# Two-layer attention and short-convolution encoder on one core: main stage of each layer put in a written order on three engines, first modulation in pairs of chunks

## The chip, the cores and the metric

The kernel runs on one core of a Trainium2 chip. The time is device microseconds of one execution. The kernel before took 310.88 us (median of three runs, 310.80 to 311.26).

## The reference

Two layers act on x (256 rows of 1024). In each layer, c (one row) is turned into a shift, a scale and a gate; x is normalised by its root mean square, scaled and shifted; one product with w_in (1024 by 4096) gives queries, keys, values and a gate for eight heads of 64, and four parts u, b, c, g of a convolution; both branches go through one product with w_out, are normalised again, gated and added to x:

```python
    for l in range(DEPTH):
        mod = c_act @ w_ada[l] + b_ada[l]
        shift, scale, gate = jnp.split(mod, 3, axis=-1)
        h = rms_norm(x, pre_norm_g[l]) * (1.0 + scale[:, None, :]) + shift[:, None, :]
        proj = h @ w_in[l]
        ...
        att = dilated_attention(q, k, v, rel_bias).astype(h.dtype) * jax.nn.silu(g_att)
        cnv = b_gate * short_conv(c_gate * u, conv_w[l]) * jax.nn.silu(g_conv)
        mix = jnp.concatenate([att, cnv], axis=-1) @ w_out[l]
        x = x + gate[:, None, :] * rms_norm(mix, post_norm_g[l])
```

Everything is fp32. In the kernel the three dilated windows become one additive bias over all 256 keys.

## The kernel before

**Products.** A large product is made of three (`mm3`, lines 234 to 239): each operand is split into a high part (a cast on ScalarE, line 145) and the rest (a subtraction on VectorE, line 146), and high by high, high by low and low by high are added in PSUM. Small products (sums for the modulation, transposes, probabilities by values) are left in plain fp32.

**First stage (layer 0, lines 413 to 506).** The order on TensorE, ScalarE and VectorE is the program's own here (`manual_schedule`). It goes over eight chunks k of 128 input columns: a row of w_in (0.92 MB, line 394) and chunk k of shift and scale from w_ada (two transfers of 0.52 MB, line 256) are loaded; `sums` (16 products, line 295, with c on 32 columns in four corners of the array) and `columns` (line 314) give the shift and scale of chunk k; `modulate` writes that chunk of h; then q, k, v and a part of the gate get their share. Within one chunk's turn the order is "q0 q1 sums k0 cols k1 g v", where sums and cols are those of the next chunk. Chunk k+1 can begin only when its cols are there.

**Main stage (lines 513 to 707 for both layers).** `split_heads` (lines 359 to 370) takes queries and keys out of PSUM for both heads of a pair. Then chunks of 256 columns of w_in are projected (u, c, b, g, a in layer 0; q, k, u, c, g, b, a in layer 1), each followed by its use; `attend(h)` (line 523) makes the scores of a head (lines 528, 529), the soft maximum (lines 534, 537), the division (lines 540, 542), four transposes (line 546), a copy to SBUF (line 548, by turns VectorE and ScalarE) and, for an odd head, the products of both heads with the values (line 554). Beside that `mods_task` makes the modulation of layer 1 and `gate_task` the gate of this layer; three of these seven sums are gathered on VectorE (`vector_sums`, lines 279 to 281) with eight short fp32 products at the end (line 287), the others on TensorE. The modulation of layer 1 is turned round through SBUF by four small transfers and one transpose (lines 569, 575). This stage has no written order: a scheduler with a timeline of its own orders each engine's queue, with heads first (`high_priority`), so splits can run ahead as far as six buffers allow.

**Between the layers (lines 757 to 811)** the order is again the program's: the last products of w_out, the second norm, the residual and the values of layer 1.

Of the kernel before, what the change touches and what calls it, by code (L numbers as in the profile page):

```python
# [10 lines left out]
F32 = mybir.dt.float32  # L11
# [4 lines left out]
P = 128  # L16
S = 256
# [51 lines left out]
def encoder_kernel(ctx, tc, x, c, w_ada, b_ada, pre_g, w_in, conv_w, rel_bias, w_out, post_g, rows, out):  # L69
# [40 lines left out]
    ones = const.tile([P, 32], F32, name="ones")  # L110
# [42 lines left out]

    def load_behind(l, c0):

        with tc.issue_after(mod_act.ins), tc.issue_after(mod_dve.ins):
            return load_cols(l, c0)
# [100 lines left out]

    def set_mods(l, k0, cols):
# [12 lines left out]
    def vector_sums(raws, pool, tag):  # L272

        for kk in range(KC // 2):
            for kh in range(2):
                k = kk + kh * (KC // 2)
                for raw in raws:
                    if kk == 0:
                        nc.vector.tensor_scalar_mul(raw[:, k], raw[:, k], c_rep[:, k, 0:1])
                    else:  # L280
                        nc.vector.scalar_tensor_tensor(raw[:, k], raw[:, k], c_rep[:, k, 0:1], raw[:, k - 1],  # L281
                                                       op0=ALU.mult, op1=ALU.add)
        g_ps = pool.tile([P, raws[0].shape[-1]], F32, name=tag)
        for kh in range(2):
            for t in range(2):
                j = 2 * kh + t
                nc.tensor.matmul(g_ps[32 * j:32 * j + 32, :], ones, raws[t][:, (kh + 1) * (KC // 2) - 1, :], start=True, stop=True)
        return take_sums(g_ps)
# [9 lines left out]
    def take_sums(g_ps, copy=nc.scalar.copy):  # L298
        acc = work.tile(list(g_ps.shape), F32, name="acc", bufs=5)
        copy(acc, g_ps)  # L300
        return acc
# [17 lines left out]
    def gate_rows(l, accs):  # L319
# [4 lines left out]
        b_row, g_row = [work.tile([2, 2, WC], F32, name=n, tag="junk", bufs=3) for n in ("b_row", "g_row")]  # L324
        nc.gpsimd.dma_start(b_row, b_ada[l, 2 * D:3 * D].rearrange("(h q n) -> h q n", h=2, q=2))
        nc.gpsimd.dma_start(g_row, post_g[l].rearrange("(h q n) -> h q n", h=2, q=2))
# [11 lines left out]
    gate_acc = {}  # L338
# [34 lines left out]
    for l in range(DEPTH):  # L373
        if l == 0:
# [38 lines left out]
            with tc.manual_schedule(engines=MANUAL):  # L413
                ada_raw = ada_load(0, 0, 1)
# [13 lines left out]
                acc = sums(ada_raw, ps, "ps", nc.vector.tensor_copy)  # L428
# [9 lines left out]
                for k in range(KC):  # L438
                    (wh, wl), (vh, vl), (gh, gl), to = next_row
                    if k == 0:  # L440
                        set_mods(0, 0, columns(acc, ps, "ps"))
                        for (a, b), w in list(zip(pieces, to))[:LEAD[0]]:
# [31 lines left out]
                    for item in (FIRST_ORDER if first else LAST_ORDER if last else ROW_ORDER).split():  # L474
# [21 lines left out]
                        elif item == "sums":  # L496
                            next_row = row_parts(k + 1)
                            acc = sums(ada_raw, ps, "ps", nc.vector.tensor_copy if first else nc.scalar.copy)
                            if not first:
                                lead_split(k + 1)  # L500
                        elif item == "lead":
                            lead_split(k + 1)
                        else:
                            set_mods(0, k + 1, columns(acc, ps, "ps"))
                sg0 = act.tile([P, 2, S], F32, name="sg0")
            nc.scalar.copy(sg0, g0_ps)
            nc.scalar.activation(warm, hT_lo[:, KC - 1, 0:1].bitcast(F32), AF.Exp, scale=0.0)
        else:
            w = load_behind(l, 0)
            q_ps = [proj_T(l, i * WC, w if i == 0 else None) for i in range(2)]  # L510
            k_ps = [proj_T(l, AW + i * WC) for i in range(2)]

        if l > 0:
            attention_tiles()
            with tc.issue_after(mod_act.ins), tc.issue_after(mod_dve.ins):
                store_values(v_ps)
        for i in range(2):
            split_heads(i, q_ps[i], k_ps[i])


        pT, turned, taken = {}, {}, {}

        def attend(h):
            o, m = h % 2, h // 2
            s_ps = ps.tile([P, NT, S], F32, name="ps")
            for t in range(NT):
                q = qkv["q"][o][:, m, t * P:(t + 1) * P]
                nc.tensor.matmul(s_ps[:, t, :], q, qkv["k"][:, o, m, :], start=True, stop=False)  # L528
                nc.tensor.matmul(s_ps[:, t, :], q, qkv["k_lo"][:, o, m, :], start=False, stop=True)  # L529
            pr_sb = work.tile([P, NT, S], F32, name="prob", bufs=3)  # L530
            mx = small.tile([P, NT], F32, name="mx", bufs=4)
            sm = small.tile([P, NT], F32, name="sm", bufs=4)
            for t in range(NT):
                nc.vector.tensor_tensor_reduce(pr_sb[:, t, :], s_ps[:, t, :], u[:, h, t * P:t * P + S][:, ::-1], scale=-1.0,  # L534
                                               scalar=3.0e38, op0=ALU.add, op1=ALU.min, accum_out=mx[:, t:t + 1])
            for t in range(NT):
                nc.scalar.activation(pr_sb[:, t, :], pr_sb[:, t, :], AF.Exp, scale=-1.0, bias=mx[:, t:t + 1],  # L537
                                     accum_out=sm[:, t:t + 1])
            rc = small.tile([P, NT], F32, name="rc", bufs=4)
            nc.vector.reciprocal(rc, sm)  # L540
            for t in range(NT):
                nc.vector.tensor_scalar_mul(pr_sb[:, t, :], pr_sb[:, t, :], rc[:, t:t + 1])
            t_ps = ps.tile([P, NT, S], F32, name="ps")
            for t in range(NT):
                for kt in range(NT):
                    turned[h] = nc.tensor.transpose(t_ps[:, kt, t * P:(t + 1) * P], pr_sb[:, t, kt * P:(kt + 1) * P], ident)  # L546
            pT[h] = work.tile([P, NT, S], F32, name="pT", bufs=3)
            (nc.vector.tensor_copy, nc.scalar.copy)[h % 2](pT[h], t_ps)
            if h % 2 == 0:
                return  # L550
            a_ps = ps.tile([P, S], F32, name="ps")
            for kt in range(NT):
                for hh in (h - 1, h):
                    taken[h] = nc.tensor.matmul(a_ps[(hh % 2) * HD:(hh % 2 + 1) * HD, :], qkv["v"][:, kt, hh * HD:(hh + 1) * HD],  # L554
                                     pT[hh][:, kt, :], start=kt == 0, stop=kt == NT - 1)
            nc.scalar.copy(qkv["o"][:, h // 2], a_ps)

        nxt = l + 1 < DEPTH

        if nxt:
            parts = const.tile([32, P], F32, name="parts")
# [266 lines left out]
```

## Time and profile before

| | |
|---|---|
| median of three runs | 310.88 us |
| the profiled execution | 311.03 us, of which the span is 309.3 us |
| TensorE busy | 300.4 us (97%) |
| VectorE busy | 211.8 us (68%) |
| ScalarE busy | 178.1 us (58%) |
| moved by DMA | 72.39 MB, mean 234 GB/s |
| mean granted TensorE clock | 0.997 |

The span runs from the first to the last instruction, 1.7 us less than the execution. Stages can be told apart by the lines that TensorE works on: warming and the first two chunks until 28 us, chunks 2 to 7 until about 65 us, the main stage of layer 0 until 158.8 us, the turn to layer 1 until 184.6 us, its main stage with the output product until 302.8 us, and the end. TensorE's time must be read by starts: a product of 256 columns lasts 0.28 us in the record, but the next one begins 0.117 us after it.

### The profile page before, as it was taken

How to read it: one execution, taken by the hardware profiler on the slowest of the kernel's cores; microseconds unless marked ns; L12 is line 12 of the kernel's file. 1: busy time of each engine (PE TensorE's matmuls, PEld its weight loads, DVE VectorE, ACT ScalarE, POOL GpSimd, SP SyncE). 2: the span in 40 equal slices, each digit the busy share in tenths (PEclk: the TensorE clock that was granted, in tenths of full speed). 3: DMA queues.
4: the chain of work that ended last, by engine and by line, in shares of the span. 5: the costliest groups of instructions: out<-in, count | busy, mean ns of one | idle time of the engine just before them, and what ended most of it. 6: DMA issues, size and time to landing. Idle time of an engine off the chain costs nothing.

```text
span 309.3 us, 6050 instructions
## 1 busy us (share of the span) xinstructions
PE 300.4 (97%) x2421; PEld 261.3 (84%) x2421; DVE 211.8 (68%) x430; ACT 178.1 (58%) x318; POOL 24.1 (8%) x49
## 2 busy tenths in 40 slices
PE   8999999999999999999999999999999999999991
PEld 6878998899877779878677899999998989998881
DVE  3554446589988498688449798798868686845333
ACT  4633445599247243989437584569637695663211
POOL 5220000000000000110013410000000001000011
PEclk9999999999999999999999999999999999999998
DMA  7999999999979999989912399758548632000002
GB/s 244 327 350 330 322 351 343 358 350 348 313 248 344 348 348 323 404 281 351 345 65 66 114 350 344 227 153 242 152 135 272 265 137 70 0 2 0 2 35 102
DMA packets 65692, 72.39 MB, mean 234 GB/s; under 512 B 1778, under 2 KB 61526, under 8 KB 65664
## 3 DMA queue, kind: packets, MB, share of 16 engines
q1 hardware_dynamic: 64512, 70.39, 70.9%
q0 software_dynamic: 784, 1.20, 1.2%
q8 instruction: 19, 0.31, 0.4%
q10 hardware_dynamic: 368, 0.42, 0.4%
q14 instruction: 9, 0.07, 0.1%
HBM read 70.91 MB, written 1.07 MB: 233 GB/s over the span
## 4 chain that ended last, share of the span: by engine, by line
PE 83%; DVE 4%; SPq 4%; DMA 3%; POOL 1%; issue 1%; ACT 1%; POOLq 0%; DVEq 0%; ACTq 0%
PE pm L237 21%; PE pm L238 21%; PE pm L239 21%; PE ps L554 4%; DMA raw<-in_w_in 3%; PE pm L295 3%; PE ps L546 3%; SPq L394 2%; PE ps L295 2%; SPq L256 2%; PE ps L238 2%; PE ps L237 2%; PE ps L239 1%; PE ps L528 1%; PE ps L529 1%
## 5 line engine op out<-in xcount | busy, mean ns | idle before, releaser
L237 PE MATMUL pm<-hT_hi,hi 128*128 128x256 f32 x408 | 116.2, 285 | 0.0
L238 PE MATMUL pm<-hT_lo,hi 128*128 128x256 f32 x408 | 114.9, 282 | 0.1
L239 PE MATMUL pm<-hT_hi,lo 128*128 128x256 f32 x408 | 114.4, 280 | 0.0
L146 DVE TENSOR_TENSOR lo<-raw,hi 128x1024 fp32r<-128x1024 f32 (+1 forms) x94 | 94.0, 1028 | 29.6 <-ACT hi L145 29.2
L145 ACT CAST hi<-raw 128x1024 fp32r<-128x1024 f32 (+1 forms) x94 | 80.5, 893 | 32.9 <-PE pm L238 15.3
L237 PEld LDWEIGHTS pm<-hT_hi,hi 128*128 128x128 f32 x408 | 76.8, 188 | 5.6 <-issue 4.5
L238 PEld LDWEIGHTS pm<-hT_lo,hi 128*128 128x128 f32 x408 | 76.8, 188 | 2.5 <-issue 1.9
L239 PEld LDWEIGHTS pm<-hT_hi,lo 128*128 128x128 f32 x408 | 76.8, 188 | 1.2 <-issue 0.8
L237 PE MATMUL pm<-hi,hT_hi 128*128 128x512 f32 (+1 forms) x68 | 23.7, 348 | 0.0
L239 PE MATMUL pm<-hi,hT_lo 128*128 128x512 f32 (+1 forms) x68 | 23.6, 346 | 0.0
L238 PE MATMUL pm<-lo,hT_hi 128*128 128x512 f32 (+1 forms) x68 | 23.3, 343 | 0.0
L537 ACT ACTIVATE prob<-prob,mx 128x256 f32<-128x256 f32 x32 | 16.0, 503 | 4.0 <-DVE mx L534 3.9
L281 DVE SCALAR_TENSOR_TENSOR raw<-raw,c_rep 128x256 f32<-128x256 f32 x36 | 16.0, 477 | 0.1
L182 ACT ACTIVATE junk<-pm 128x512 f32<-128x512 f32 (+1 forms) x9 | 5.0, 550 | 17.2 <-PE pm L239 17.1
L239 PEld LDWEIGHTS pm<-hi,hT_lo 128*128 128x128 f32 x68 | 12.8, 188 | 2.2 <-DVE hT_lo L231 0.6
L237 PEld LDWEIGHTS pm<-hi,hT_hi 128*128 128x128 f32 x68 | 12.8, 188 | 2.0 <-DVE hT_hi L230 0.4
L724 DVE TENSOR_TENSOR og<-pm,gg 128x512 f32<-128x512 f32 (+1 forms) x9 | 5.6, 630 | 12.7 <-ACT junk L182 12.7
L238 PEld LDWEIGHTS pm<-lo,hT_hi 128*128 128x128 f32 x68 | 12.8, 188 | 1.3
L554 PE MATMUL ps<-pT,v_sb 128*64 128x256 f32 x64 | 13.8, 398 | 0.0
L238 PE MATMUL pm<-lo,mix_a 128*128 128x512 f32 (+1 forms) x36 | 13.4, 373 | 0.0
L237 PE MATMUL pm<-hi,mix_a 128*128 128x512 f32 (+1 forms) x36 | 13.4, 372 | 0.0
L239 PE MATMUL pm<-hi,mix_a 128*128 128x512 f32 (+1 forms) x36 | 12.7, 371 | 0.0
(176 smaller groups left out, 446.0 us busy)
## 6 DMA issues: line engine op xcount, KB each, us to landing
raw<-in_w_in SPq DMA_DIRECT2D x25, 1024.0 KB, 7.6
raw<-in_w_ada SPq DMA_DIRECT2D x16, 1024.0 KB, 10.8
raw<-in_w_ada SPq DMA_DIRECT2D x16, 512.0 KB, 8.4
raw<-in_w_out SPq DMA_DIRECT2D x8, 1024.0 KB, 6.9
raw<-in_w_in SPq DMA_DIRECT2D x7, 896.0 KB, 10.0
u<-t_dr SPq DMA_DIRECT2D x1, 1536.0 KB, 10.0
x_sb<-in_x SPq DMA_DIRECT2D x2, 512.0 KB, 4.3
gg<-r_dr POOLq DMA_DIRECT2D x2, 512.0 KB, 4.2
```

Of the source, the lines that this page charges most:

```text
L145: nc.scalar.copy(hi, raw)
L146: nc.vector.tensor_sub(lo, raw, hi.bitcast(F32))
L237: nc.tensor.matmul(o, ah, bh, start=first, stop=False, **kw)
L238: nc.tensor.matmul(o, ah, bl, start=False, stop=False, **kw)
L239: return nc.tensor.matmul(o, al, bh, start=False, stop=last, **kw)
L256: nc.sync.dma_start(raw[:, t], w_ada[l].rearrange("(k p) n -> p k n", p=P)[:, :, t * D + k0 * P:t * D + (k0 + n) * P])
L281: nc.vector.scalar_tensor_tensor(raw[:, k], raw[:, k], c_rep[:, k, 0:1], raw[:, k - 1], op0=ALU.mult, op1=ALU.add)
L295: nc.tensor.matmul(g_ps[32 * j:32 * j + 32, :], c_rep[:, kk + kh * (KC // 2), :], raws[t][:, kk + kh * (KC // 2), :], start=kk == 0, stop= ...
L394: row_dma[0] = nc.sync.dma_start(raw[:, a:b], w_in[0, k * P:(k + 1) * P, a:b])
L537: nc.scalar.activation(pr_sb[:, t, :], pr_sb[:, t, :], AF.Exp, scale=-1.0, bias=mx[:, t:t + 1], accum_out=sm[:, t:t + 1])
L546: turned[h] = nc.tensor.transpose(t_ps[:, kt, t * P:(t + 1) * P], pr_sb[:, t, kt * P:(kt + 1) * P], ident)
L554: taken[h] = nc.tensor.matmul(a_ps[(hh % 2) * HD:(hh % 2 + 1) * HD, :], qkv["v"][:, kt, hh * HD:(hh + 1) * HD], pT[hh][:, kt, :], start=kt ...
```

## The change

The main stages of both layers get a written order on TensorE, ScalarE and VectorE (SyncE's and GpSimd's queues stay with the scheduler). A chunk is worked in two halves, the units j = 0, 1, 2 and so on (24 in layer 0, 34 in layer 1), each 24 products. For each j the loop emits: sums that are due; the values of a pair (`take`); scores; transposes (`turn`); the division; what `PLAN` lists; the split of unit j+2; the soft maximum; loads; the products of unit j; their use. Head h starts at unit `HEAD_AT[l][h]`; its division comes one unit later, its transposes two, and an odd head's values three. All seven sums are on TensorE; the columns of the modulation of layer 1 come from `columns`, two chunks each time, without the small transfers. All copies of turned probabilities go to ScalarE.

In the first stage shift and scale are loaded and summed for chunks 0, 1, 2+3 and 4+5; for 6+7 VectorE gathers them in eight steps of 512 elements (four after the splits of chunk 4, four after those of chunk 5), and `columns_of` turns the result.

```diff
-GATE_AT = ((0, 3), (None, 1))
-ROWS_AT = (6, 5)
-MODS_AT = (1, 2, 4, 5)
-HEAD_AT = ((2, 2, 3, 4, 5, 6, 6, 7), (0, 0, 1, 2, 3, 4, 5, 6))
+UNITS = ("u0 u1 c0 c1 b0 b1 g0 g1 a1 o0 o1 o2", "q0 k0 q1 k1 u0 u1 c0 c1 g0 g1 b0 b1 a0 a1 o0 o1 o2")
+LOADS = ("u1 c0 s0 c1 b0 s1 b1 r0 g0 s2 g1 r1 a1 s3 o0 o1 o2 o3", "q0 k0 q1 k1 u0 u1 r1 c0 c1 g0 g1 b0 b1 a0 a1 o0 o1 o2 o3")
+HEAD_AT = ((2, 4, 6, 8, 10, 12, 14, 16), (6, 8, 11, 13, 16, 18, 21, 23))
+PLAN = ({0: "=heads0", 1: "=heads1 =copy0", 5: "<sums0", 6: "=cols0", 7: "<sums1", 8: "=cols1 =taps0", 9: "<gate0 =taps1",
+         10: "=taps2", 11: "<sums2 =taps3", 12: "=cols2 =line0", 13: "<gate1", 15: "<sums3", 16: "=cols3 =rows0", 17: "=conv0 >side0",
+         18: "=conv1 =att0", 19: ">att1"},
+        {1: "=store0", 4: "=heads0", 8: "=heads1 =line0", 11: "<gate1", 13: "=rows0", 16: "=taps0", 17: "=taps1", 18: "=taps2",
+         19: "=taps3", 24: "=conv0", 25: "=conv1", 28: "=att0", 29: "=att1"})
+AHEAD = 2
+ADA_GROUPS = ((0, 1, -1), (1, 1, 0), (2, 2, 1), (4, 2, 3), (6, 2, 4))
...
+    def chain(raws, acc):
...
+        for k, (raw, j) in enumerate(steps):
+            part = raw[..., j, :]
+            if k == 0:
+                nc.vector.tensor_scalar_mul(part, part, c_rep[:, k, 0:1])
+            else:
+                nc.vector.scalar_tensor_tensor(acc if k == KC - 1 else part, part, c_rep[:, k, 0:1], before,
+                                               op0=ALU.mult, op1=ALU.add)
...
-                    if k + 1 < KC:
-                        ada_raw = ada_load(0, k + 1, 1)
+                    for f, n, at in ADA_GROUPS[1:]:
+                        if at == k:
+                            ada_raw[f] = ada_load(0, f, n) if f < 6 else ada_halves(0, f)
...
+                    if k in (4, 5):
+                        if k == 4:
+                            last_chain = chain(ada_raw[6], last_acc)
+                        for _ in range(KC // 2):
+                            next(last_chain)
...
-                            acc = sums(ada_raw, ps, "ps", nc.vector.tensor_copy if first else nc.scalar.copy)
+                            if k + 1 in ada_raw and k + 1 < 6:
+                                acc = sums(ada_raw[k + 1], ps, "ps", nc.vector.tensor_copy if first else nc.scalar.copy)
...
-                        else:
+                        elif k + 1 == 6:
+                            set_mods(0, 6, columns_of([last_acc[:, t] for t in range(2)], ps, "ps"))
+                        elif k + 1 in ada_raw:
                             set_mods(0, k + 1, columns(acc, ps, "ps"))
...
+        with tc.manual_schedule(engines=MANUAL):
...
+            def turn(h):
...
+                nc.scalar.copy(pT[h], t_ps)
...
+            for j, (name, m) in enumerate(units):
+                stage = {j - at: h for h, at in enumerate(HEAD_AT[l])}
+                late = PLAN[l].get(j, "").split()
+                for what in [w for w in late if w[0] == "<"]:
+                    does[what[1:-1]](int(what[-1]))
+                if 3 in stage and stage[3] % 2:
+                    take(stage[3])
+                if 0 in stage:
+                    scores(stage[0])
+                if 2 in stage:
+                    turn(stage[2])
+                if 1 in stage:
+                    divide(stage[1])
+                for what in [w for w in late if w[0] == "="]:
+                    does[what[1:-1]](int(what[-1]))
+                if j + AHEAD < len(units):
+                    split_unit(*units[j + AHEAD])
+                if 0 in stage:
+                    softmax(stage[0])
+                load_more()
...
+                    out_unit(name, m)
+                else:
+                    project(name, m)
+                    if m:
+                        use(name)
+                for what in [w for w in late if w[0] == ">"]:
+                    does[what[1:-1]](int(what[-1]))
+            load_more()
+            w1, w2 = [[parts_of[n, m] for m in range(2)] for n in ("o1", "o2")]
+            w = [split(raws["o3"][:, m, :], [P, D]) for m in range(2)]
```

In `PLAN`, heads0 and heads1 are `split_heads(0)` and `split_heads(1)`, unchanged; s0 to s3 are the sums of the modulation of layer 1, r0 and r1 those of the gate, conv and att the splits of the two branches for the output product, copy0 and side0 the copy and the activation of the gate part that the first stage made.

## Rows read from the trace of the kernel before

**Rows 1.** The page: busy time by engine, and the chain that ended last, by engine.

```profile
PE 300.4 (97%) x2421; PEld 261.3 (84%) x2421; DVE 211.8 (68%) x430; ACT 178.1 (58%) x318; POOL 24.1 (8%) x49
...
PE 83%; DVE 4%; SPq 4%; DMA 3%; POOL 1%; issue 1%; ACT 1%; POOLq 0%; DVEq 0%; ACTq 0%
```

**Rows 2.** Stretches: length, busy PE, PEld, DVE, ACT, POOL, PEclk, DMA share, GB/s.

```profile
28.00:61.50 33.50, 33.43 (x357) 29.90 (x358) 18.12 (x44) 15.71 (x33) 0.00 (x0) 1.00 1.10 342
61.50:158.80 97.30, 97.30 (x768) 80.97 (x767) 75.04 (x152) 61.40 (x109) 4.08 (x7) 1.00 0.99 325
...
184.60:280.20 95.60, 95.60 (x783) 89.34 (x782) 72.77 (x136) 62.80 (x101) 1.17 (x2) 1.00 0.51 165
```

**Rows 3.** Timeline of TensorE, first stage: start, us, instruction, idle before in brackets.

```profile
22.90 1.07 PE L295 MATMUL ps<-raw,c_rep 128*32 128x128 f32 x30 [0.16 <-DMA raw<-in_w_ada]
...
27.85 0.39 PE L237 MATMUL pm<-hT_hi,hi 128*128 128x256 f32 x1
28.30 0.38 PE L238 MATMUL pm<-hT_lo,hi 128*128 128x256 f32 x1
...
29.79 1.08 PE L295 MATMUL ps<-raw,c_rep 128*32 128x128 f32 x32
...
31.61 0.28 PE L314 MATMUL ps<-pair,acc 128*128 128x2 f32 x2
```

**Rows 4.** Timeline of TensorE, main stage of layer 0.

```profile
91.86 1.93 PE L295 MATMUL pm<-raw,c_rep 128*32 128x256 f32 x30
...
98.27 0.28 PE L237 MATMUL pm<-hT_hi,hi 128*128 128x256 f32 x1
...
98.50 0.28 PE L239 MATMUL pm<-hT_hi,lo 128*128 128x256 f32 x1
98.71 1.08 PE L554 MATMUL ps<-pT,v_sb 128*64 128x256 f32 x6
```

**Rows 5.** Stretches, busy PE of one line: L295; L287 in both layers; L554.

```profile
61.50:158.80 97.30, 10.19 (x128) 4.20 (x128) 1.00 0.99 325
...
61.50:158.80 97.30, 2.94 (x16) 0.71 (x16) 1.00 0.99 325
184.60:280.20 95.60, 0.64 (x8) 0.16 (x8) 1.00 0.51 165
...
61.50:158.80 97.30, 6.89 (x32) 2.65 (x32) 1.00 0.99 325
```

**Rows 6.** Groups by line and shape: count, busy us, mean ns of one, idle before.

```profile
L146 DVE TENSOR_TENSOR lo<-raw,hi 128x1024 fp32r<-128x1024 f32 x64 | 77.0, 1222 | 21.8 <-ACT hi L145 21.4
...
L145 ACT CAST hi<-raw 128x1024 fp32r<-128x1024 f32 x64 | 65.4, 1050 | 28.6 <-PE pm L238 15.3 <-DMA raw<-in_w_in 7.2 <-PE pm L239 2.2
L537 ACT ACTIVATE prob<-prob,mx 128x256 f32<-128x256 f32 x32 | 16.0, 503 | 4.0 <-DVE mx L534 3.9
...
L534 DVE CUSTOM_DVE_ANT_0 prob<-ps,u 128x256 f32<-128x256 f32 x32 | 12.2, 420 | 0.3
...
L537 ACT ACT_TABLE_LOAD x5 | 6.4, 1283 | 0.1
...
L729 DVE SCALAR_TENSOR_TENSOR x_sb<-og,rstd,x_sb 128x512 f32<-128x512 f32 x7 | 5.0, 748 | 1.5 <-POOL rstd L194 1.5
```

**Rows 7.** Timelines of ScalarE and VectorE, heads of layer 1, idle before in brackets.

```profile
200.73 0.60 ACT L363 ACTIVATE q_odd<-pm 64x512 fp32r<-64x512 f32 x1 [0.93 <-DVE q_even L364]
...
207.18 0.58 ACT L368 CAST k_hh<-pm 64x512 fp32r<-64x512 f32 x1 [1.78 <-DVE k_low L370]
...
215.22 0.69 DVE L370 TENSOR_TENSOR k_low<-pm,k_hh 64x512 fp32r<-64x512 f32 x1 [0.76 <-ACT k_hh L369]
```

**Rows 8.** TensorE's first products (timeline), and a stretch after its last one.

```profile
1.48 3.78 PE L381 MATMUL ps<-zeros 128*128 128x256 f32 x8 [1.48 <-DVE zeros L109]
...
5.39 2.72 PE L381 MATMUL ps<-zeros 128*128 128x256 f32 x8
...
307.00:308.00 1.00, 0.00 (x0) 0.00 (x0) 0.00 (x0) 0.00 (x0) 0.00 (x0) 0.63 0.51 168
```

More of the change, by code (lines that the diff above doesn't have):

```diff
@@ L298, in take_sums @@
     def take_sums(g_ps, copy=nc.scalar.copy):
-        acc = work.tile(list(g_ps.shape), F32, name="acc", bufs=5)
+        acc = work.tile(list(g_ps.shape), F32, name="acc", bufs=6)
         copy(acc, g_ps)
@@ L513, in encoder_kernel @@
[L513 to L544, printed above, removed]
-                for kt in range(NT):
[L546 to L556, printed above, removed]
@@ L609, in encoder_kernel @@
-        running = []
-        step = [0]
-        def side():
-            for h in heads[step[0]]:
-                with tc.high_priority(1000):
-                    attend(h)
-            running.extend(starts[step[0]])
-            step[0] += 1
-            for t in list(running):
-                try:
-                    next(t)
-                except StopIteration:
-                    running.remove(t)
-        def chunk(c0, use, w=None, pool=pm):
-            use(proj_T(l, c0, w, pool))
-            side()
@@ L704, in encoder_kernel, with mix_k @@
-        side()
-        while running or any(starts[step[0]:]) or any(heads[step[0]:]):
-            side()
-        w = load_out(l, OUT_K[3])
+                        out_k(t, parts_of[name, m], k, n, k == OUT_K[0], False)
+            def mix_k(k, ts_):
+                if k < 4:
+                    return hT_hi[:, k, ts_], hT_lo[:, k, ts_]
+                return cv["mix"][:, 0, k - 4, ts_], cv["mix"][:, 1, k - 4, ts_]
+            cuts = [[slice(0, 512), slice(512, 1024)] for _ in range(NT)]
@@ new lines, in encoder_kernel, with out_k, out_pair @@
+            if not nxt:
+                cuts[1][1:] = [slice(512, 768), slice(768, 1024)]
+            def out_k(t, w, k, n, first, last):
+                cs = cuts[t][n]
+                mm3(o_ps[t][n], mix_k(k, slice(t * P, (t + 1) * P)), (w[0][:, cs], w[1][:, cs]), first, last)
+            def out_pair(w, k0, ts):
+                for kk in range(2):
+                    for t in ts:
+                        for n in range(len(cuts[t])):
+                            out_k(t, w[kk], k0 + kk, n, k0 + kk == OUT_K[0], False)
@@ new lines, in heads_in, with lines @@
+            def heads_in(i):
+                if l == 0:
+                    split_heads(i, q_ps[i], k_ps[i])
+                else:
+                    split_heads(i, pending[f"q{i}"], pending[f"k{i}"])
+            def lines(_):
+                cv["lines"] = gate_lines(l)
+            does = {"heads": heads_in, "taps": taps, "conv": conv_split, "att": gate_heads, "sums": mods_sums, "cols": mods_cols,
+                    "gate": gate_sums, "line": lines, "rows": lambda _: gate_rows(l, gates[l], *cv["lines"]),
+                    "copy": lambda _: nc.scalar.copy(sg0, pending["g0"]), "store": lambda _: store_values(pending["v"]),
+                    "side": lambda i: gate_of(i, sg0)}
```

329 lines of the change are left out of this document (189 added, 140 removed).

## The prediction

> **What bounds the kernel now.** I read the page first, then stretches, then the timeline of TensorE by starts. TensorE is busy 97% of the span and holds 83% of the chain that ended last [rows 1]. The stretches show how evenly: from 28 to 158.8 us and from 184.6 to 280.2 us it has no idle time worth naming [rows 2]. In those stretches the records also follow each other without holes: products of 256 columns start 0.117 us apart (two steps from 98.27 to 98.50), and a change between the three-part products and plain fp32 costs about 0.1 us on each side [rows 4]. So only two things can move the time: TensorE's own work, and new waits of TensorE. VectorE (75.0 of 97.3 us in the main stage of layer 0) and ScalarE (61.4) are not full [rows 2]; they matter by the order in which they do things. DMA moves 342 GB/s in the first stage, at a share over 1 [rows 2], and there TensorE already finds one transfer just arriving (0.16 us idle at 22.90) [rows 3].
>
> The sum is made against the profiled execution, 311.03 us (span 309.3), 0.15 above the median.
>
> **First stage, TensorE's work.** Sums of chunks 3, 5, 6 and 7 go: each is 1.0 us and 0.2 for two changes of kind, so -4.8. The sums for 2+3 and 4+5 are twice as wide: by duration 1.93 against 1.08 [rows 3, 4], +0.85 each, +1.7. Columns (0.14 to 0.28 for a pair [rows 3]) are eight turns before and ten after in fewer places: 0. Together -3.1.
>
> **First stage, waits.** (a) The sums for chunk 2 wait for their slice of w_ada. The queue to them now carries 1.05 MB more: 1.05 / 0.342 = 3.1 us [rows 2]. Nothing on TensorE hides it, since that transfer is only just in time today and the sums stand ahead of half of chunk 1's products. Bounds: 0 (the queue had slack) and 3.1; I take 3.0, nearest the row with the idle time. The present 0.16 and the 0.45 at 27.85 (instead of 0.1) [rows 3] go, -0.6: splits and h will be early there. (b) VectorE's chain for chunks 6+7: eight steps of 512 elements at most 0.75 each (the same operation in the residual) [rows 6], 0.7 back to back, 2.8 for four. The second four stand behind the splits of chunk 5, which end about 1.5 us after TensorE starts on that chunk. So they end near 4.3, while TensorE asks for the columns after 18 products, at 2.1: +2.1. Bounds 0 and 3. First stage: -3.1 + 3.0 - 0.6 + 2.1 = **+1.4**.
>
> **Main stages, TensorE's work.** Values: 6.89 us a layer, four pairs, each in two pieces [rows 5]; a piece of six lasts 1.08 [rows 4], so eight in one piece 1.3. Saved 6.89 - 4 x 1.3 = 1.7 a layer. Sums, layer 0: 10.19 + 2.94 today [rows 5] against six of 2.04 (1.93 for 30 instructions [rows 4]): -0.9, and three share their changes of kind with values, -0.6. Columns for layer 1: +1.1, the transpose that goes -0.2. Layer 0: **-2.3**. Layer 1: -1.7 for values, +1.4 for the sums that leave VectorE (2.04 against 0.64 [rows 5]), -0.5 for shared changes: **-0.8**.
>
> **What costs nothing.** VectorE loses three sums, ScalarE gains eight copies (0.6 each): over two main stages neither bounds. GpSimd's queue loses the four small transfers of the modulation, and issues the two loads for the gate's rows four units ahead of the row products instead of with them; the broadcast that follows is used some 20 us later, after the output product, so it stays covered (uncovered it would cost its own few us once a layer). SyncE's loads follow the same six buffers; each slice of layer 0 is asked for at least one unit before its split, by the order of `LOADS`; if that cover is gone, a slice costs 3.1 us.
>
> **Main stages, new waits.** Today the scheduler puts splits ahead of the heads. In the written order `split_heads` stands in one piece on ScalarE and VectorE, and the unit after next is split behind it. Its steps alternate: ScalarE's second step waits for VectorE's first, on another tile but the same PSUM source (0.93 and 1.78 us idle), and VectorE for ScalarE's last (0.76) [rows 7]. In one piece that is 0.6 + 0.7 + 0.6 + 1.2 + 0.7 + 1.2 = 5.0 us of ScalarE for a pair, though it is busy 3.5. Below, ScalarE's and VectorE's splits take 1.05 and 1.2, two maxima 0.8, two exponentials 1.1, a table 1.3 [rows 6], a division 0.8, a copy 0.6.
>
> *Layer 0, start.* Zero is TensorE's first product of chunk 7. It reaches unit 0 at 4.9, the scores of head 0 at 10.5, unit 2 at 11.0, unit 3 at 13.8. ScalarE copies v until 2.0, loads the table until 3.5, then heads0 until 8.5, the split of unit 2 until 9.5, heads1 until 15.1 (VectorE first ends that split), a copy until 15.7, unit 3 until 16.7, VectorE's half until 17.9. Unit 3 waits 3.9. Behind it the maxima end at 20.3, the exponentials at 21.5, the division at 22.3, while TensorE wants to turn head 0 at 21.0: 1.3 more. **+5.2** (0.5 if the pair cost only 3.5).
>
> *Layer 0, end.* After g1 ScalarE has activations, the soft maximum of head 7 with a table, another table for the gate, the splits of both branches and of six units. Zero at unit 16: the copy of head 7 ends at 11.5 (TensorE wants it at 11.0, 0.5 lost); the split of o2 comes behind the heads' split, 20.1 and 21.3, wanted at 19.0 (2.3 lost); o1 and o3 lose 0.5 more. **+3.3** (bounds 1 and 4.5).
>
> *Layer 1, start.* heads0 at unit 4 delays the split of unit 6: +1.0. At unit 8 the order on ScalarE is copy, heads1, split of unit 10, exponentials of head 1. From TensorE's start of unit 8: copy until 1.6, heads1 6.6, split 7.7 (VectorE 8.9), maxima 9.7, exponentials 10.8, division 11.6. TensorE has two units and reaches the turn of head 1 at 6.6: +5.1. **+6.1** (3.6 if the pair cost 3.5, 0 if splits and exponentials were not behind it).
>
> **Sum:** 1.4 - 2.3 - 0.8 + 5.2 + 3.3 + 6.1 = +12.9; 311.0 + 12.9 = 323.9, less 0.15: 323.8, say **323.5**, since waits in a row hide a little of each other.
>
> [...]
>
> **The rivals.**
> *Waits stay hidden, TensorE remains the bound (faster).* The pieces of ScalarE overlap better than I read, or TensorE's reserve of split units covers them. Then the main stages give 2.3 + 0.8 back, the first stage costs its 1.4 or less: 309.2; with the first stage's waits hidden too, 304.6. For it: VectorE loses two sums in layer 0, and ScalarE has 36 us free there (97.3 - 61.4) [rows 2]. Against: reserve is two units, 5.6 us, and heads1 with a split takes more.
> *The pair costs 3.5.* If the alternation of [rows 7] came from other work in the queues, layer 0's start costs 0.5 and layer 1's 3.6: 316.6. Against: three separate waits end within 0.05 us of the other engine's end.
> [...]
> *The order does not bind:* SyncE and GpSimd stay with the scheduler, so loads could come late; that adds to the slow side only.
>
> **How the numbers follow.** Chances: forecast 0.45, clock falls 0.1, pair at 3.5 with waits between 312 and 319 0.18, waits hidden 0.2, and 0.07 that savings and waits meet at no change. About 0.2% (0.6 us) is what can be told from no change here. Faster 0.2, same 0.07, slower 0.73. The range takes 308.0 to 327.0: below it lies half of the rival that is faster, above it the clock's drop with a further wait. The forecast's own range is 318 to 327, by the bounds of its three places.
>
> **What would show it.** In the new profile: TensorE idle or stretched at the sums of chunk 2 (about 3 us, released by DMA) and at the columns of chunk 6 (about 2 us, by VectorE); at unit 3 of layer 0 (by VectorE's split) and at the turn of head 1 in layer 1 (by the division); eight L554 products in one row of 1.3 us. ScalarE's row of L363 and L368 should show VectorE as releaser before every second step. I am wrong if TensorE's busy time stays whole through both main stages, or if heads1 is passed in 3.5 us.

## The result and the profile after

The changed kernel takes 326.05 us (median of 4 executions, 325.26 to 327.98) against 311.05 for the kernel before: a ratio of 1.049, 95% interval 1.045 to 1.054. Slower, as forecast; 2.5 us above the forecast of 323.5 and inside its range. The profiled execution took 325.26 us, 14.2 more than the one of before; it is the fastest of the four (mean clock 0.981, the others 0.971 to 0.975). Its page, busy time, granted clock in 40 slices and chain:

```profile
PE 299.1 (93%) x2384; PEld 264.5 (82%) x2384; DVE 195.6 (61%) x383; ACT 174.5 (54%) x318; POOL 21.1 (7%) x45
...
PEclk9999998999999999999999989999799999999998
...
PE 65%; DVE 11%; ACT 11%; issue 4%; DMA 4%; SPq 4%; POOL 1%; DVEq 0%; ACTq 0%; POOLq 0%
```

TensorE falls from 97% to 93% of the span, and VectorE and ScalarE, 4% and 1% of the chain before [rows 1], hold 11% each. TensorE no longer runs through. Its timeline shows each place (start, us, instruction; in brackets the idle time before and what ended it):

```profile
24.97 1.93 PE L315 MATMUL ps<-raw,c_rep 128*32 128x256 f32 x30 [1.38 <-DMA raw<-in_w_ada]
...
53.03 0.80 PE L307 MATMUL ps<-ones,acc_last 128*128 128x1 f32 x6 [2.52 <-DVE acc_last L296]
...
78.89 0.39 PE L242 MATMUL ps<-hT_hi,hi 128*128 128x256 f32 x1 [1.70 <-ACT hi L155]
...
80.15 0.39 PE L244 MATMUL ps<-hT_hi,lo 128*128 128x256 f32 x1 [0.76 <-DVE lo L156]
...
83.76 0.44 PE L585 MATMUL ps<-ident,prob 128*128 128x128 f32 x2 [0.31 <-DVE prob L578]
...
158.53 0.49 PE L242 MATMUL pm<-hi,hT_hi 128*128 128x512 f32 x1 [0.65 <-ACT hi L155]
159.79 0.50 PE L243 MATMUL pm<-lo,hT_hi 128*128 128x512 f32 x1 [0.77 <-DVE lo L156]
...
183.43 1.28 PE L836 MATMUL ps<-ident,xhat 128*128 128x128 f32 x8 [1.99 <-DVE xhat L873]
...
188.08 0.39 PE L242 MATMUL pm<-hi,hT_hi 128*128 128x256 f32 x1 [0.81 <-DVE hT_hi L235]
...
227.97 0.73 PE L585 MATMUL ps<-ident,prob 128*128 128x128 f32 x4 [4.40 <-DVE prob L578]
...
234.82 1.08 PE L593 MATMUL ps<-pT,v_sb 128*64 128x256 f32 x8
```

Read downwards: sums of chunk 2, columns of chunk 6, unit 3 (twice) and the turn of head 0 in layer 0, the first half of o2 (twice), the layer turn (twice), and the turn of head 1 in layer 1; the last line, values in one piece, is used further below. Where the rows of before have 0.16 and 0.45 [rows 3], there is now a chain of waits, ended by the other engines. Stretches of the same execution (length, busy PE, PEld, DVE, ACT, POOL, then PEclk, DMA share, GB/s):

```profile
54.50:57.80 3.30, 3.30 (x14) 3.01 (x13) 2.54 (x7) 3.19 (x7) 0.00 (x0) 0.50 1.10 348
184.20:187.50 3.30, 3.06 (x15) 2.77 (x13) 3.30 (x4) 1.65 (x5) 1.89 (x2) 0.50 1.05 341
228.55:231.90 3.35, 3.35 (x18) 3.35 (x17) 2.20 (x2) 1.75 (x3) 0.00 (x0) 0.50 0.29 67
```

After three of the waits the granted clock is 0.50 for about 3.3 us, although TensorE is busy. The first and the third stretch cost about half their length, some 1.5 us each (e2 and e5 below). The second costs nothing, for VectorE has three splits to end before the part of h that TensorE needs next:

```profile
184.33 3.49 DVE L156 TENSOR_TENSOR lo<-raw,hi 128x1024 fp32r<-128x1024 f32 x3
187.73 0.29 DVE L235 CAST hT_hi<-h 128x256 fp32r<-128x256 f32 x1
```

In e2 the clock is at full in this stretch. TensorE is busy for 1.48 us of it instead of 3.06, and then waits 2.04 us instead of 0.81:

```profile
184.20:187.50 3.30, 1.48 (x12) 1.28 (x11) 3.30 (x4) 1.69 (x5) 1.90 (x2) 1.00 1.06 350
```

```profile
187.73 0.38 PE L242 MATMUL pm<-hi,hT_hi 128*128 128x256 f32 x1 [2.04 <-DVE hT_hi L235]
```

From the transposes to this product it is 4.65 us in the changed kernel (183.43 to 188.08) and 4.66 in e2 (183.07 to 187.73). So some 3 us of half clock stand in no wait.

Two places explain the most. ScalarE at the start of layer 0, and ScalarE, then VectorE, before the turn of head 1 in layer 1:

```profile
65.55 0.59 ACT L386 ACTIVATE q_even<-pm 64x512 fp32r<-64x512 f32 x1 [0.82 <-PE pm L244]
...
70.51 1.05 ACT L155 CAST hi<-raw 128x1024 fp32r<-128x1024 f32 x1
71.58 0.59 ACT L386 ACTIVATE q_even<-pm 64x512 fp32r<-64x512 f32 x1
...
76.70 0.58 ACT L392 CAST k_hh<-pm 64x512 fp32r<-64x512 f32 x1
...
79.21 1.06 ACT L155 CAST hi<-raw 128x1024 fp32r<-128x1024 f32 x1
...
218.48 0.59 ACT L386 ACTIVATE q_even<-pm 64x512 fp32r<-64x512 f32 x1
...
222.95 0.58 ACT L392 CAST k_hh<-pm 64x512 fp32r<-64x512 f32 x1
223.44 1.04 ACT L155 CAST hi<-raw 128x1024 fp32r<-128x1024 f32 x1
226.24 0.51 ACT L569 ACTIVATE prob<-prob,mx 128x256 f32<-128x256 f32 x1 [1.76 <-DVE mx L566]
```

```profile
224.51 1.23 DVE L156 TENSOR_TENSOR lo<-raw,hi 128x1024 fp32r<-128x1024 f32 x1 [0.25 <-ACT hi L155]
...
227.56 0.62 DVE L578 TENSOR_SCALAR prob<-prob,rc 128x256 f32<-128x256 f32 x2
```

A pair of heads takes 5.1 us of ScalarE (65.55 to 70.6) and 5.05 again in layer 1 (218.48 to 223.5). Behind it stand, one after another, the split of unit 10, the maxima, the exponentials and the division that the turn waits for.

### The profile page after: what moved, and what is told of

Read it like the earlier page. It is cut to its first block, busy times and chain, and to the rows that moved or that the text cites. A ratio compares the mean times of both kernels' runs of the same rounds, so it can differ in the third digit from the quotient of the medians.

```text
span 322.9 us, 5883 instructions
## 1 busy us (share of the span) xinstructions
PE 299.1 (93%) x2384; PEld 264.5 (82%) x2384; DVE 195.6 (61%) x383; ACT 174.5 (54%) x318; POOL 21.1 (7%) x45
## 4 chain that ended last, share of the span: by engine, by line
PE 65%; DVE 11%; ACT 11%; issue 4%; DMA 4%; SPq 4%; POOL 1%; DVEq 0%; ACTq 0%; POOLq 0%
PE pm L242 17%; PE pm L243 16%; PE pm L244 16%; DVE lo L156 4%; PE pm L315 4%; DMA raw<-in_w_ada 4%; ACT hi L155 4%; SPq L417 2%; PE ps L593 2%; PE ps L585 2%; DVE raw L296 1%; PE ps L556 1%; PE ps L315 1%; ACT k_hh L392 1%; PE ps L557 1%
## 5 line engine op out<-in xcount | busy, mean ns | idle before, releaser
L242 PE MATMUL pm<-hT_hi,hi 128*128 128x256 f32 x408 | 117.4, 288 | 0.0
L243 PEld LDWEIGHTS pm<-hT_lo,hi 128*128 128x128 f32 x408 | 77.6, 190 | 0.3
L244 PEld LDWEIGHTS pm<-hT_hi,lo 128*128 128x128 f32 x408 | 77.6, 190 | 0.1
L587 ACT COPY pT<-ps 128x512 f32<-128x512 f32 x16 | 9.4, 587 | 22.0 <-PE ps L585 22.0
L242 PEld LDWEIGHTS pm<-hi,hT_hi 128*128 128x128 f32 x68 | 13.5, 199 | 3.9 <-DVE hT_hi L235 1.1
L315 PE MATMUL pm<-raw,c_rep 128*32 128x256 f32 x256 | 15.7, 382 | 0.0
L243 PEld LDWEIGHTS pm<-lo,hT_hi 128*128 128x128 f32 x68 | 13.5, 199 | 2.3 <-DVE lo L156 1.1
L244 PEld LDWEIGHTS pm<-hi,hT_lo 128*128 128x128 f32 x68 | 13.5, 199 | 1.8 <-DVE hT_lo L236 0.2
L585 PE MATMUL ps<-ident,prob 128*128 128x128 f32 x64 | 9.8, 276 | 4.7 <-DVE prob L578 4.7
```

Source lines behind the costliest of these rows:

```text
L242: nc.tensor.matmul(o, ah, bh, start=first, stop=False, **kw)
L243: nc.tensor.matmul(o, ah, bl, start=False, stop=False, **kw)
L244: return nc.tensor.matmul(o, al, bh, start=False, stop=last, **kw)
L315: nc.tensor.matmul(g_ps[32 * j:32 * j + 32, :], c_rep[:, kk + kh * (KC // 2), :], raws[t][:, kk + kh * (KC // 2), :], start=kk == 0, stop= ...
L587: nc.scalar.copy(pT[h], t_ps)
```

## The experiments

In diffs a minus is the changed kernel. "Scores to output" is the time in the profile from TensorE's first scores of a layer to its first output product.

**e1: the first stage as before.**

```diff
-ADA_GROUPS = ((0, 1, -1), (1, 1, 0), (2, 2, 1), (4, 2, 3), (6, 2, 4))
+ADA_GROUPS = ((0, 1, -1),) + tuple((k, 1, k - 1) for k in range(1, KC))
```

(and without `chain` and `columns_of`)

> Undoes the first stage's part alone: the first modulation is loaded, summed and applied chunk by chunk as before, with no chain on VectorE; the main stages stay as changed (326.05 us). Theory: the pairs cost 3.2 us where the first stage ends (chunk 7 starts at 63.25 instead of 60.05), namely the wait at the sums of chunk 2 (1.6), the wait for the chain before the columns of chunk 6 (2.7) and the half clock after it (1.6), less some TensorE work. So 322.9 us, the clock at full in the first stage, and the two later drops and all waits of the main stages as they are. Rival 1: a late start is taken up by waits of the main stages, which are set by other engines: 326 us. Rival 2: the blind term for this stage was right and the rest is chance: 1.4 us, so 324.6 us.

327.89 us (326.71 to 329.76), ratio 1.055: not faster at all, so rival 1. But the first stage did what the theory said: the first scores start at 70.15 instead of 73.75. What followed took it back (timeline of TensorE, then a stretch):

```profile
78.15 0.58 PE L242 MATMUL ps<-hT_hi,hi 128*128 128x256 f32 x1 [3.15 <-ACT hi L155]
```

```profile
77.00:83.70 6.70, 5.09 (x22) 4.79 (x23) 4.64 (x11) 4.56 (x9) 0.00 (x0) 0.50 0.57 190
```

TensorE came 3.6 us earlier to the first scores, but ScalarE ends the second pair of heads only 0.7 us earlier. A wait of 0.76 us appears at unit 2, the one at unit 3 grows from 1.70 to 3.15 us, so that unit 3 starts 0.7 us earlier (78.15 instead of 78.89), and behind it the clock is at 0.50 for the 6.7 us of this stretch; in the changed kernel's profile it is at 1.00 there. By the turn of head 0 this version is 0.8 us behind. So the first stage's cost was real and yet lay, for the most part, under a later wait: the terms of my sum do not add.

**e2: heads1 in layer 1 taken apart.**

```diff
-8: "=heads1 =line0"
+7: "=hq1", 8: "=line0 +ka1", 9: "+kb1"
```

(`hq` is the q half; `ka` and `kb` are k of the even and the odd heads; `+` stands behind the unit's split)

> In layer 1 alone the split of the second head pair is taken apart: its q half in unit 7, behind the division of head 0; half of k in unit 8, behind the split of unit 10; the other half in unit 9, behind the split of unit 11. Theory: the 4.6 us wait of TensorE at the turn of head 1 is the 5.0 us of this piece standing ahead of the split, the maxima, the exponentials and the division, and the 3.4 us at half clock behind it are its consequence (1.7 us lost). Both go: 326.05 - 4.6 - 1.7 = 319.8 us, with at most 0.7 us left at that place and no clock drop at 228.5. Rival 1: the pieces only move the wait, to the split of unit 11 or the scores of head 2: 324 to 326 us. Rival 2: the division is late by the split of unit 10 alone (2.3 us): then under 1.5 us is gained and the drop stays, 324.5 us.

320.95 us (319.97 to 324.62). The theory holds: of the 4.4 us at the turn of head 1 less than 0.5 is left, the clock there stays at 1.00, and scores to output in layer 1 takes 77.4 us instead of 83.25, 5.9 less where 6.3 was expected. The execution of 324.62 had a mean clock of 0.969, the three others 0.978 to 0.980.

**e3: first splits of layer 1 behind the layer turn.**

```diff
+            with tc.issue_after(mod_act.ins), tc.issue_after(mod_dve.ins):
                 for j in range(AHEAD):
                     split_unit(*units[j])
```

> The first splits of layer 1 are issued on ScalarE and VectorE behind the last modulation of the layer turn, as the function that the change took out had them. Theory: in the changed kernel three such splits stand on ScalarE ahead of the sum of squares of the second half of x (180.85 instead of about 178.9) and on VectorE ahead of the split of h (187.7 instead of about 185.2); this makes the waits of 2.25 us before the transposes and of 1.1 us in the values products, and the half clock from 184.1 to 187.6 (1.7 us). They go: a gain of 4 to 4.8 us, 321.2 to 322 us, with the clock at full through the turn. Rival 1: the reciprocal root on GpSimd or the residual on VectorE sets that end, as before the change (0.9 us there): gain under 1 us, 325 to 326. Rival 2: layer 1 then starts without its split units, so that q0 waits 2 us or more: gain 2 us, 324.

324.75 us (323.97 to 325.99). In the profile the wait before the transposes shrinks by 1.2 us, the second wait and the half clock in the turn are gone, and from the first transposes of the turn to the first scores of layer 1 it takes 35.7 us instead of 38.55: 2.8 gained, 4 expected, as wait and half clock overlapped. ScalarE in the changed kernel, then in this one:

```profile
178.01 2.96 ACT L155 CAST hi<-raw 128x1024 fp32r<-128x1024 f32 x3
180.85 0.64 ACT L187 ACTIVATE junk<-x_sb 128x512 f32<-128x512 f32 x1
```

```profile
181.93 0.64 ACT L187 ACTIVATE junk<-x_sb 128x512 f32<-128x512 f32 x1 [0.75 <-DVE x_sb L817]
...
189.85 2.94 ACT L155 CAST hi<-raw 128x1024 fp32r<-128x1024 f32 x3
```

Three splits of the next layer stood ahead of the sum of squares on which the turn depends. The median moved by 1.3 us only; in the profiled execution (325.99, mean clock 0.971 against 0.981) the clock fell in four places, two of which the changed kernel's profile does not have.

**e4: order in layer 0.**

```diff
-1: "=heads1 =copy0", 5: "<sums0"
+1: "=copy0", 3: "+hq1", 4: "+ka1", 5: "<sums0 +kb1"
-19: ">att1"
+20: ">att1"
```

> In layer 0 alone: the split of the second head pair is taken apart (q in unit 3, half of k in unit 4, half in unit 5, each behind the split of its unit) and the gating and splitting of the last two head pairs goes one unit later, behind the split of o2's first half. Theory: the waits at unit 3 (1.9 and 0.9 us) and at the turn of head 0 (0.5) come from the two pairs' 5 us pieces ahead of the split of unit 3, and the waits at o2 (0.8 and 1.0) from that gating ahead of its splits, which only o3 needs. All go: 326.05 - 3.3 - 1.8 = 320.9 us; the clock drops are elsewhere and stay. Rival 1: unit 3 waits for its slice of weights, not for the order: only 1.8 us gained, 324.2. Rival 2: what is saved in layer 0 is spent in waiting for transfers that then come too late (they move 368 GB/s up to here): 324 to 326.

Profiled 319.53 us, 5.7 under the changed kernel's; median 323.27 (to 324.0), with mean clocks of 0.969 to 0.975 in the other executions against 0.985. The waits at unit 3 and at the turn of head 0 are gone. Of the two at o2, the first shrank from 0.65 to 0.37 us and the second (0.8 us, for VectorE's split) stayed. Rival 1 falls, for unit 3 no longer waits. Not all of the 5.7 us is the edit's: the first scores come 1.4 us earlier (72.35 instead of 73.75), as the clock does not fall in the first stage this time. From there to the transposes of the layer turn it takes 106.0 us instead of 109.7, so 3.7 gained where 5.1 were expected.

**e5: work in the wait.**

```diff
+if (l, h) == (1, 1):
+    for _ in range(18):
+        nc.tensor.matmul(t_ps[:, 0, 0:P], ident, ident, start=True, stop=True)
```

> The changed kernel, with 18 more products of the identity by itself (128 columns, their result is overwritten) on TensorE right before the turn of head 1 in layer 1, that is in the 4.6 us for which it waits there. Nothing else is moved: the turn still comes when VectorE has divided. Theory: the half clock after that wait (228.5 to 231.9) follows from TensorE doing nothing in it and costs 1.7 us; with work in the wait it stays at full there, the turn comes at the same distance from the scores, and the output products of layer 1 start 83.25 - 1.7 = 81.5 us after its first scores. Whole time 326.05 - 1.7 = 324.4 us, if the drops elsewhere are the same. Rival 1: the drop is of its own and comes all the same: 83.2 us, 326. Rival 2: the added products are longer than the wait and delay the turn: over 83.3 us, 326.5.

324.56 us (323.26 to 326.15). The turn of head 1 comes 17.16 us after the first scores, as in the changed kernel (17.17), so nothing was delayed. The stretch behind it:

```profile
228.60:232.00 3.40, 3.40 (x34) 3.12 (x36) 2.31 (x2) 1.87 (x3) 0.00 (x0) 1.00 0.30 57
```

34 products where the changed kernel has 18 in 3.35 us, at clock 1.00. From the turn to the first output product it takes 64.56 us instead of 66.08: 1.5 us. The drop stood behind this wait in all five profiles that have it bare, at 4.4 us (the changed kernel, e1, e3, e4 and e6). So the half clock follows from TensorE doing nothing here, and 1.5 us is its price.

**e6: splits three units ahead.**

```diff
-AHEAD = 2
+AHEAD = 3
```

> The changed kernel with splits three units ahead instead of two, in both layers, and the written order otherwise as it is. Theory (order, not capacity): waits on a split go, since each split then stands a unit earlier in its queues, ahead of the heads: unit 3 of layer 0 (1.9 and 0.9 us) and part of o2 (0.8). The wait at the turn of head 1 in layer 1 stays, for the maxima and the division still stand behind heads1: 4.6 us and its drop. 326.05 - 3.6 = 322.5 us. Rival 1: ScalarE and VectorE are simply too full here, so that a longer reserve only moves the waits: 325 to 327. Rival 2: splits further ahead take the place of softmax steps, and the turns of the heads come later in several places: 327 to 330.

327.14 us (326.06 to 328.39): no gain. The wait at unit 3 is gone and a longer one stands at the turn of head 0 (timeline of TensorE):

```profile
85.38 0.70 PE L585 MATMUL ps<-ident,prob 128*128 128x128 f32 x4 [3.30 <-DVE prob L578]
```

From the first scores to this turn it takes 10.01 us, as in the changed kernel (75.37 to 85.38 and 73.75 to 83.76). ScalarE has the same list before the exponentials of head 0: two pairs of heads with a split between them, and two more splits (16.48 us from the first pair on, and 16.47 in the changed kernel). By its time this lies at the border of the two rivals; by its profile it is the first, for a longer reserve has only moved the wait.

**c1, c2: the mended main stages, with pairs and without.** c1 is e2, e3 and e4 together; c2 adds e1.

> The pieces of the second head pair in both layers, the gating of the last two pairs one unit later in layer 0, and the first splits of layer 1 behind the layer turn, together; the first modulation in pairs of chunks is kept. Theory: the waits are at separate places and add: by the profiles, 5.9 (layer 1), 2.8 (layer turn) and 5.1 (layer 0) off the profiled 325.3 give 311.5 us; what is left over the sum of TensorE's own savings (3 us in the main stages) is the first stage's 3.2 us and a wait of 1 us at o2. Rival 1: an earlier wait covers a later one, as the first stage's did: 314 to 317. Rival 2: every wait left still lets the clock fall, in places that change: 313 to 316.

> The same with the first modulation chunk by chunk as before. When the first stage alone was undone, the first scores came 3.6 us earlier, but TensorE waited that much longer for unit 3, whose split is set by ScalarE's and VectorE's order, and the clock fell for 6.8 us. Theory: with the pieces in place nothing is left there to wait for, so the 3.2 us of the first stage now show in the whole: 308.3 us, under the 311.0 of the kernel before, and the clock is at full throughout. Rival 1: the first stage's end is set by something that the pairs relieve elsewhere, or the gain goes into the next wait again: 311 to 312. Rival 2: the pairs' saved products (3.1 us of TensorE's work) outweigh their waits once the rest is mended: slower than the version with pairs.

c1: 313.73 us (312.63 to 315.02), ratio 1.008, interval 1.005 to 1.011; the profiled 312.63 is 1.1 over what the theory gave. That theory took 5.1 us for layer 0 from e4's profile, of which 1.4 were the clock in the first stage; with 3.7 it gives 312.9. In the profile its only half clock before the end stands behind the columns of chunk 6 (54.80 to 58.2, at 0.50). c2: 310.66 us (310.56 to 312.02), ratio 1.000 (0.998 to 1.001), clock at full until the end (mean 0.995). So by the medians the first stage is worth 3.1 us here: theory 3.2, against nothing in e1. By the two profiles c2 reaches the first scores 3.8 us earlier (70.21 against 74.01), c1's half clock included, and the turn of head 0 2.4 us earlier (78.16 against 80.57); a new wait at unit 2 is part of the difference. The forecast of 308.3 was missed by 2.4, about the size of the waits for splits that are left in layer 0 (0.9 at unit 2, 0.5 and 1.0 at o2, by the spacing of the products); c5 tries them.

**c5, c6: two places more, and the pairs without the chain.** In this diff a minus is c2; c6 is c5 with pairs of chunks, all summed on TensorE.

```diff
-{0: "=heads0", 1: "=copy0"
+{0: "=hq0 +ka0", 1: "=kb0 =copy0"
-if j + AHEAD < len(units):
-    split_unit(*units[j + AHEAD])
+more = [j + AHEAD] if l or j < 13 else [15, 16] if j == 13 else [j + AHEAD + 1]
+for n in more:
+    if n < len(units):
+        split_unit(*units[n])
```

> The mended kernel with the first modulation chunk by chunk (310.7 us) and two places more in layer 0: the first head pair is split as q, then the split of unit 2, then k of the even heads (all that head 0 needs), the rest of k in unit 1; and from unit 13 on splits go three units ahead, where ScalarE and VectorE are idle for 2 to 3 us. Theory: TensorE's waits at unit 2 (0.9 us) and in o2 (0.5 and 1.0 us) are again splits behind something that is not yet needed, so they go: 310.66 - 2.4 = 308.3 us, a ratio of 0.992. Rival 1: at the end of layer 0 VectorE has more work than time (six splits of 1.2 us and the gating in 8 us), so an earlier split only shifts the wait: 309.5 to 310. Rival 2: what is won before the layer turn is lost in it, since its 1.0 us wait is set by GpSimd and VectorE: 310.5.

> The same as c5_more, but with the first modulation in pairs of chunks, the sums of the last pair on TensorE as those of the others instead of in the chain on VectorE. Of the first stage's two waits it keeps the one for the slice of w_ada (2.5 us at the sums of chunk 2) and takes away the one for the chain (2.7 us, with a drop of the clock behind it, 1.7). Theory: the slice for two chunks arrives 2.5 us later because the queue carries 1.05 MB more ahead of it; against this stand about 0.9 us fewer products for sums than chunk by chunk: 308.3 + 2.5 - 0.9 = 309.9 us, with no wait at chunk 6. Rival 1: the transfer only arrives late because the program asked late, and wins back later: 308. Rival 2: the drop of the clock comes after the wait that is left, 1.7 more: 311.6.

c5: 309.6 us, ratio 0.9945 (0.992 to 0.997), 1.1 gained of 2.4. Three waits went; 0.3 us at o2 stayed, two of 0.45 came at turns of heads, and the profiled execution waits 1.5 us for its first slice of w_ada. c6: 309.53 us, the same. Its ten executions stand in two groups: five at 308.6 to 309.0 us with a mean clock of 0.994 to 0.997, five at 310.1 to 310.4 with 0.988 to 0.990. The profiled one is of the second group, and shows why (timeline, then a stretch):

```profile
25.02 2.98 PE L315 MATMUL ps<-raw,c_rep 128*32 128x256 f32 x30 [2.28 <-DMA raw<-in_w_ada]
```

```profile
25.80:29.10 3.30, 3.30 (x27) 1.83 (x20) 0.09 (x1) 0.89 (x2) 0.00 (x0) 0.50 1.02 374
```

The clock is at half after the wait for the slice. The groups differ by 1.5 us, as in e5. With the chain off VectorE, pairs are no worse than single chunks. From c1 to c6 it is 4.2 us, of which the two places more are worth 1.1 (c2 to c5). That leaves 3.1 for the chain with what it does to the clock; no run takes the chain away alone.

**c7, c8: two ways around the wait for the slice**, both from c6.

```diff
c7: -(2, 2, 1), (4, 2, 3), (6, 2, 4)
    +(2, 1, 1), (3, 1, 2), (4, 2, 3), (6, 2, 4)
c8: in chunk 1 "q0 q1 k0 k1 sums g cols v" for "q0 q1 sums k0 cols k1 g v"
```

> The version with pairs summed on TensorE (309.5 us, or 308.7 in the executions without a drop of the clock and 310.2 in those with one), but chunks 2 and 3 one by one; only 4+5 and 6+7 are pairs. Theory: the wait of 2.5 us at the sums of chunk 2 comes from asking for two chunks at once where each transfer is only just in time; later pairs are asked for two chunks ahead and showed no wait. So the wait and the drop behind it go, for about 0.4 us more of products for sums: 308.7 - 2.5 + 0.4 = 306.6 us, all executions near each other, a ratio of 0.986. Rival 1: the queue is late at chunk 3 or 4 instead, since the bytes until then are nearly the same: 308 to 309, with drops. Rival 2: later waits take up what the first stage wins: 309.

> Pairs throughout on TensorE, with 2+3 as in the change, but in chunk 1 the sums stand behind both halves of k instead of ahead of them, so that 1.4 us of products cover a part of the wait for the transfer. Theory: if the transfer is what is late, the wait shrinks from 2.5 to 1.1 us: 308.7 - 1.4 = 307.3 us, and no clock drop: all executions near 307.3. Rival 1: what follows the sums (columns, modulation, h of chunk 2) then stands ahead of chunk 2 with too little cover, and a wait of 1 to 2 us appears before its first product: 308.5 to 309. Rival 2: the transfer itself is late because a buffer comes free late, which is set by the products, so that the wait keeps its length: 308.7.

c7: 309.22 us (308.6 to 309.43), 2.6 over the theory. The wait at chunk 2 and the drop are gone (mean clocks 0.994 to 0.998), but 0.46 and 0.39 us appear at the start of chunk 5, for the splits of its weights, and the profiled execution waits 1.8 us for its first slice, where c8's waits 0.4. Whether that belongs to c7 or to the one execution isn't settled. c8: 308.26 us (308.12 to 308.4), ratio 0.992 (0.990 to 0.993): the fastest here, 0.8% under the kernel before. It is 1.0 us over its theory, and 0.5 under the five executions of c6 with the higher clock (308.75 in the middle). The two waits that its theory and its first rival name, in TensorE's timeline:

```profile
25.13 1.93 PE L315 MATMUL ps<-raw,c_rep 128*32 128x256 f32 x30 [0.62 <-DMA raw<-in_w_ada]
...
30.11 0.38 PE L242 MATMUL pm<-hT_hi,hi 128*128 128x256 f32 x1 [0.32 <-DVE hT_hi L235]
```

All four executions lie within 0.3 us, and TensorE runs through the main stages again, as in [rows 2]:

```profile
68.00:161.00 93.00, 92.72 (x792) 79.17 (x792) 60.03 (x122) 56.77 (x106) 2.05 (x5) 1.00 0.92 299
...
180.00:277.40 97.40, 97.35 (x833) 92.70 (x834) 64.48 (x114) 60.38 (x102) 1.18 (x2) 1.00 0.54 174
```

## Why the prediction was right, and where it was not

The verdict and its cause stand: TensorE was full, ScalarE and VectorE were not, and the written order made TensorE wait for them. e2, e4 and c1 show it by taking waits away with the order alone. Idle times below are the brackets of the timeline.

| step of the forecast | forecast, us | measured, us |
|---|---|---|
| slice for the sums of chunk 2 | 3.0 | 1.4 |
| chain before the columns of chunk 6 | 2.1 | 2.5 |
| unit 3 and the turn of head 0 | 5.2 | 2.8 |
| end of layer 0 | 3.3 | 1.4 |
| layer turn | none | 2.8, where before had 0.6 |
| heads0 in layer 1 | 1.0 | 0 |
| heads1 in layer 1 | 5.1 | 4.4 |
| values of a layer, from 6.89 [rows 5] | 5.2 | 4.3 and 4.5 |
| half clock | none (a chance of 0.1) | 4.9, of which some 3 lengthen the run |

**The pair of heads** was forecast at 5.0 us of ScalarE and took 5.1; the rival of 3.5 falls. That it alternates with VectorE could be read before, from three waits [rows 7]; that is why unit 3 and the turn of head 1 were named in advance.

**The chain:** VectorE's splits of chunk 5 come first and the last four steps behind them, as forecast:

```profile
47.64 2.23 DVE L156 TENSOR_TENSOR lo<-raw,hi 128x512 fp32r<-128x512 f32 x4
49.78 2.32 DVE L296 SCALAR_TENSOR_TENSOR raw<-raw,c_rep 128x512 f32<-128x512 f32 x3
52.13 0.75 DVE L296 SCALAR_TENSOR_TENSOR acc_last<-raw,c_rep 128x512 f32<-128x512 f32 x1
```

**Sizes that were off.** For the start of layer 0 the step was "ScalarE copies v until 2.0, loads the table until 3.5". The table is loaded before the copy, at a time when ScalarE waits for TensorE anyway:

```profile
59.45 1.28 ACT L545 ACT_TABLE_LOAD x1
...
64.15 0.58 ACT L379 COPY v_sb<-pm 128x512 f32<-128x512 f32 x1 [1.31 <-PE pm L244]
```

So heads0 begins 2.3 us after TensorE's start on chunk 7 (63.25), not 3.5, and the two waits behind it are 1.4 and 1.0 us shorter. At the end of layer 0 the copy of head 7 was in time, and o1 did not wait. At the slice for chunk 2 the queue had some slack, for which 3.0 left none (1.4 us in this profile; 1.9 to 2.3 in those of e3 to e6, c1 and c6). Values in one piece take 1.08 us, no longer than six of the eight did [rows 4].

**Terms that do not add.** The sum took the first stage's cost as time of its own. e1 shows that most of it lay under the wait at unit 3, whose end ScalarE and VectorE set. "Waits in a row hide a little of each other" got 0.3 us; here it was 2.9 of the 3.6 us.

**The step that failed: the clock.** A fall of the clock had a chance of 0.1 and a share in the upper end of the range, "the clock's drop with a further wait". The cost taken for it was my estimate, which no run shows; in its place the runs showed 1.5 us for a drop that lengthens the run (e5, and the two groups of c6). In the profile three falls follow waits of 2.5, 2.0 and 4.4 us. Two of them lengthen the run, by some 3 of the 14.2 us; the one in the layer turn only shortens the wait behind it.

**The step that was missing: the layer turn.** The diff takes out `load_behind`, which held the first splits of layer 1 behind the last modulation. I priced it at nothing without naming its cover, counting only splits that come too late; here splits came too early, and e3 gives 2.8 us back.

**Luck in the size.** TensorE's own work shrank by 6.2 us, as forecast (busy 299.1 us, of which 4.9 are half clock, against 300.4). But the waits that the sum priced came to 12.5 us against 19.7. What it left out made up for these 7.2: the layer turn 2.2 more than before, and 4.9 of TensorE's busy time by the half clock. That the time came within 2.5 us of the point is due to these errors meeting, not to each size being right.

The rivals: *waits stay hidden* was wrong in every place but heads0 in layer 1, where the reserve of two units did cover. The fall of the clock did come, in three places, and 0.1 was far too low a chance for it.

What the change itself is worth: in c8 its parts (three engines in written order, values in one piece, pairs of chunks) save 2.6 us over the kernel before. The change as first written cost 15.

## What to carry to other kernels

An order written by hand for an engine that is not the bottleneck needs, for each long piece, the list of what stands behind it and who waits for that; a piece that alternates between two engines is cut so that the next unit's split and the next softmax pass between. Look also for what an edit lets come too early, not just too late. And when a wait is taken away, look whether the next one grows instead: alone the first stage gave nothing (e1), with the rest mended 3.1 us (c2 against c1).

## What the runs showed of the hardware

The same wait of TensorE, 2.5 us for the chain, was followed by 3.3 us at half clock in some profiles and not in others. In c6 five of ten executions are 1.5 us longer at a lower mean clock, and the profiled one of these has the drop after the wait for the slice. Of the seven profiles with the 2.52 us wait for the chain, five show the drop behind it, and e2 and e4 do not. In e2 the wait before the columns of chunk 6 is 2.52 us, as in the changed kernel, and the stretch after it is at full:

```profile
53.02 0.91 PE L307 MATMUL ps<-ones,acc_last 128*128 128x1 f32 x7 [2.52 <-DVE acc_last L296]
```

```profile
54.50:57.80 3.30, 3.30 (x25) 3.03 (x24) 2.54 (x7) 3.20 (x7) 0.00 (x0) 1.00 1.10 348
```

25 instructions in the time in which the changed kernel did 14, and first scores 1.56 us earlier (72.19 instead of 73.75). Where the time of an execution is longer, its mean clock is mostly lower (e4: 0.985 at 319.53 us, 0.969 to 0.975 at 322.6 to 324.0). So it is likely that the changed kernel and e1 to e6 spread by 0.6 to 1.5% between executions for this reason, and c8 by 0.1%. The drop in the layer turn cost nothing (4.65 us with it, 4.66 in e2 without): TensorE had to wait for VectorE there in any case. The change of a median between two such versions says little; the profile's own stages say more.
